# A hybrid decoder layer on one core: first expert index compared inside the sums, one-hot rows made by ACT, sample turns spread, first norm's gain on turned rows

## The chip, the cores and the metric

The kernel runs on one core of one Trainium2 chip. A core has a matrix engine (PE, with its weight loads shown as PEld), a vector engine (DVE), an activation engine (ACT), a general engine (POOL) that also issues the gathers, and SP, whose queue issues the plain DMAs. The metric is the device time of one execution in microseconds, the median of three: 2513.51 us before the change (2503.61 to 2522.33).

## The reference

One layer runs over 256 prompt tokens and over 8 x 4 sample tokens. The first half (projections, RWKV recurrence, sparse attention, output projection) isn't touched but for its end. What follows it:

```python
h = jnp.concatenate([y_r, y_n], axis=-1) @ p['w_out']
x = layer_norm(DEEPNORM_ALPHA * x + h, p['ln1_g'], p['ln1_b'])
f = peer_ffn(x, p['peer_wq'], p['peer_subkeys'], p['peer_u'], p['peer_v'])
x = layer_norm(DEEPNORM_ALPHA * x + f, p['ln2_g'], p['ln2_b'])
...
q = (xt @ wq).reshape(n, P_HEADS, 2, P_DKEY // 2)            # 8 heads, 2 halves of 128
s = jnp.einsum('nhcd,hckd->nhck', q, subkeys)                # 128 keys for each half
hv, hix = lax.top_k(s, P_TOPK)                               # 16 of 128
cand = (hv[:, :, 0, :, None] + hv[:, :, 1, None, :]).reshape(n, P_HEADS, 256)
cand_e = (hix[:, :, 0, :, None] * N_KEYS + hix[:, :, 1, None, :]).reshape(n, P_HEADS, 256)
tv, tpos = lax.top_k(cand, P_TOPK)
expert = jnp.take_along_axis(cand_e, tpos, axis=-1)          # 8 x 16 experts of 16384 a token
gate = jax.nn.softmax(tv, axis=-1)
h = jax.nn.gelu(jnp.einsum('cd,chkd->chk', xb, u_tab[eb]), approximate=False)
out = jnp.einsum('chk,chkd->cd', gb * h, v_tab[eb])
```

D is 2048, all in float32. An expert's number is 128 times a first index plus a second index, each 0 to 127.

## The kernel before

The program is written as stages; a scheduler sets the order of the instructions on each engine from its own estimate of times, held by priorities, by "issue after" marks and, in the weigh stage, by the order in which the source pins them. Tiles live in pools: a tile can be written when the tiles of its memory have been read for the last time, so the order in which pools open and close decides when a load may start. The stages that matter, with the times of the profiled execution:

- W4 (765 to 983 us): the prompt's attention, the first half of the output product (`out_first`, L1678), and the sample tokens' whole chain (`sample_chain`, L1465): their norm, queries, choice of experts, and their 64 gathered rows of `peer_u`, half a row of 1024 numbers each, in `cw` tiles, each multiplied and summed on DVE by one SCALAR_TENSOR_TENSOR with an accumulator (L1552, "sample dots").
- out (983 to 1062): the second half of the output product (`out_part(8, YN)`, L1647), with the sample dots woven into it (`weave((chain, 32), ...)`). DVE adds the product to x (L1676).
- ln1 (1062 to 1103): `layer_norm` (L1622) on 2 x 128 prompt tokens: bn_stats, a Newton rsqrt of small DVE steps for one block of tokens at a time, ACT's scaling of the rows (L1633), the gain on DVE (L1634), the bias half on POOL and half on DVE (L1635). PE turns the finished rows (L1727) and ACT copies them to `XT` (L1731). SP writes the rows to `X1D` in memory.
- wq (1103 to 1239): 16 column blocks of the query product (L1808, 32 matmuls each), ACT's copy to `QP` (L1809), scores (L1375) per head. `choose` (L1386) finds the best 16 of 54 candidate sums on DVE; POOL makes the candidates' numbers CE from HF and multiplies the hit mask by them (L1410); `settle` (L1413) adds the hits on DVE and writes the expert's number as an integer into GI, on DVE (L1417).
- peer/dense (1239 to 1713): for each first index i1, `dense` (L1837) multiplies 9 x 128 columns of x by the 128 experts' columns of u (AW holds all 16384 sums). The other 896 columns are gathered row by row for the chosen experts and summed on DVE (`dot`, L1771, one L1777 instruction a slot of 128 tokens, 256 slots in all). Gathered rows go through five tiles named `rows` (NRW = 5).
- weigh (1713 to 1982): 68 steps over 64 groups u of four tokens. `pick` (L1878): DVE compares an iota with both indices at once (`oo`, 128x1024), PE turns the second index's one-hot rows (tile pt) and ACT copies them (`oT`). `picked` (L1891): PE takes AW's rows (px). `product_of` (L1897): DVE multiplies px with the first index's one-hot rows and sums (four L1905 a step), ACT's Gelu every second step. `scaled` (L1915): ACT scales the first index's one-hot rows by the gate (four L1918). `put` (L1920): PE makes pa from the second index's rows and the scaled rows, ACT copies it into AW. In steps 0 to 27 the last 58 dots run. In steps 28 to 59 the sample's 64 gathers of `peer_v` go through the `rows` tiles, two a turn, and PE adds them into fs (L1942, eight matmuls a turn). After the steps the sample's second norm runs (its loads L1984 and L1986, L1987 on), and its 16 stores leave by SP (L1991).
- V (1982 to 2497): for 128 first indices k, `rows_load` (L1950) brings 1408 columns of v, ACT and DVE split them (L2034, L2035), PE multiplies by AW (L2042, 18 matmuls a k). The other 640 columns are gathered (`rq`) and added on DVE (L2015). From k = 66 on, every sixth k issues one load of the last norm's rows into AW's first half, which is read until then (L2056, L2060).

## Time and profile before

| stage | from, us | to, us | what bounds most of it |
|---|---|---|---|
| W4 | 765 | 983 | PE 202.82 of 218 busy |
| out | 983 | 1062 | DVE 70.96 and PE 59.73 of 79 |
| ln1 | 1062 | 1103 | DVE 37.00 of 41, PE 7.74 |
| wq | 1103 | 1239 | PE 123.42 and DVE 109.61 of 136 |
| dense | 1239 | 1713 | PE 462.09 of 474 |
| weigh, steps 0 to 27 | 1713 | 1840 | DVE 122.70 of 127 |
| weigh, the rest | 1840 | 1982 | PE 131.71 of 142 |
| V | 1982 | 2497 | PE 497.22 of 515 |

The profiled execution took 2521.09 us, its span 2518.9 us, and its mean granted clock of the matrix engine was 0.929. A stage's table says how long each engine was busy; whether an engine sets the stage's time is read from the waits and from the chain of work that ended last. An operation's mean time in a group holds its overlap with its neighbours, so for a row of many the busy time over the count is its pitch.

### The profile page before, as it was taken

The numbers are of one execution on the slowest core, as the hardware profiler recorded it, in microseconds if no ns is written. First come the engines' busy times: TensorE is split into PE (matmuls) and PEld (weight loads), VectorE is DVE, ScalarE is ACT, GpSimd is POOL, SyncE is SP. The second block draws the span as 40 slices with busy tenths as digits, with TensorE's granted clock in tenths as the row PEclk, the third lists the DMA queues.
The fourth block names the chain that finished last, engine by engine and source line by source line (L and its number), as shares of the span: only waits on it lengthen the run. The fifth ranks groups of instructions, "written<-read, shape, count | busy, mean of one in ns | idle before, by whom it ended". The sixth has DMA issues, their size and how long they took to land.

```text
span 2518.9 us, 44857 instructions
## 1 busy us (share of the span) xinstructions
...
## 2 busy tenths in 40 slices
...
GB/s 225 223 234 227 270 219 168 118 177 228 168 233 252 282 278 170 344 293 182 134 340 371 370 372 351 357 353 227 205 241 291 219 364 359 361 367 353 359 365 198
DMA packets 327420, 683.17 MB, mean 271 GB/s; under 512 B 82206, under 2 KB 200928, under 8 KB 326400
## 3 DMA queue, kind: packets, MB, share of 16 engines
...
q14 instruction: 91, 0.75, 0.1%
...
## 4 chain that ended last, share of the span: by engine, by line
PE 50%; DVE 17%; DMA 9%; POOL 9%; issue 8%; ACT 3%; SPq 1%; POOLq 0%; DVEq 0%; ACTq 0%
PE ph L1850 10%; PE pb L2042 10%; POOL rq L454 6%; PE pj L423 5%; PE ph L1843 3%; PE p L1080 2%; PE pa L1668 2%; DVE rows L1777 2%; PE pa L1924 2%; DVE ul L1640 2%; DMA co<-in_cache_cmp_kv,gidx 2%; PE pj L1808 1%; DVE cw L1552 1%; PE px L1894 1%; PE sa L921 1%
## 5 line engine op out<-in xcount | busy, mean ns | idle before, releaser
L454 POOL DMA_INDIRECT rq<-in_peer_v_g,gi x256 | 404.3, 1579 | 118.0 <-DVE fP L2015 67.8
L454 POOL DMA_INDIRECT rows<-in_peer_u_g,gi x256 | 327.0, 1277 | 249.5 <-DVE rows L1777 206.8
L1777 DVE SCALAR_TENSOR_TENSOR rows<-rows,x1a 128x896 f32<-128x896 f32 x256 | 274.3, 1100 | 2.0 <-DMA rows<-in_peer_u_g,gi 1.9
L423 PE MATMUL pj<-XH,wl 128*128 128x288 f32 (+1 forms) x752 | 231.8, 309 | 13.9 <-DVE wl L418 7.7
L423 PE MATMUL pj<-XH,wh 128*128 128x288 f32 (+1 forms) x752 | 229.7, 306 | 14.0 <-DVE ss L753 6.1
L1850 PE MATMUL ph<-XHd,uh 128*128 128x256 f32 x768 | 236.4, 308 | 0.0
L1850 PE MATMUL ph<-XHd,ul 128*128 128x256 f32 x768 | 224.6, 293 | 8.4 <-DVE ul L1640 3.6
L1640 DVE TENSOR_TENSOR ul<-ur,uh 128x384 fp32r<-128x384 f32 x256 | 133.6, 560 | 128.1 <-ACT uh L1639 88.1
L423 PE MATMUL pj<-XL,wh 128*128 128x288 f32 (+1 forms) x752 | 225.9, 301 | 0.0
L2015 DVE SCALAR_TENSOR_TENSOR fP<-rq,ge,fP 128x640 f32<-128x640 f32 x254 | 223.7, 881 | 2.4
L1850 PE MATMUL ph<-XLd,uh 128*128 128x256 f32 x768 | 217.0, 283 | 0.0
L2042 PE MATMUL pb<-vl,ah 128*128 128x512 f32 (+1 forms) x768 | 206.9, 378 | 0.0
L2042 PE MATMUL pb<-vh,ah 128*128 128x512 f32 (+1 forms) x768 | 187.7, 380 | 20.8 <-ACT vh L2034 20.8
L2042 PE MATMUL pb<-vh,al 128*128 128x512 f32 (+1 forms) x768 | 205.8, 376 | 0.0
L416 ACT CAST wh<-wraw 128x512 fp32r<-128x512 f32 (+1 forms) x188 | 115.0, 616 | 227.0 <-PE pj L423 188.3
L1843 PE MATMUL ph<-Xfd,ur 128*128 128x256 f32 x768 | 187.3, 379 | 2.4 <-DMA ur<-in_peer_u_t 2.4
L2042 PEld LDWEIGHTS pb<-vh,ah 128*128 128x128 f32 x768 | 142.9, 191 | 44.5 <-ACT vh L2034 21.9
L477 DVE SCALAR_TENSOR_TENSOR CA<-co,wbc,CA 128x256 f32<-128x256 f32 x248 | 135.6, 585 | 48.5 <-DMA co<-in_cache_cmp_kv,gidx 48.5
L1850 PEld LDWEIGHTS ph<-XHd,ul 128*128 128x128 f32 x768 | 146.5, 191 | 22.7 <-DVE ul L1640 22.0
L423 PEld LDWEIGHTS pj<-XH,wl 128*128 128x128 f32 (+1 forms) x752 | 143.9, 191 | 25.7 <-DVE wl L418 11.6
L1852 ACT COPY AW<-ph 128x256 f32<-128x256 f32 x128 | 77.8, 608 | 217.4 <-PE ph L1850 204.8
L423 PEld LDWEIGHTS pj<-XH,wh 128*128 128x128 f32 (+1 forms) x752 | 144.2, 192 | 20.7 <-ACT wh L416 6.7
...
## 6 DMA issues: line engine op xcount, KB each, us to landing
ur<-in_peer_u_t SPq DMA_DIRECT2D x128, 576.0 KB
...
wraw<-in_w_in SPq DMA_DIRECT2D x64, 128.0 KB
...
```

The costliest lines, as they stand in the source:

```text
L416: sc.copy(wh[:, :, :n], w[:, :, :n])
L423: last[2] = pe.matmul(pb[:n, :nt], wi[:, k, :n], xi[(o + k) // 8][:, (o + k) % 8, :nt], start=(o + k == 0 and wi is wh and xi is xh), stop ...
L454: gp.indirect_dma_start(out=dst, out_offset=None, in_=rows_, in_offset=bass.IndirectOffsetOnAxis(ap=ix, axis=0))
L477: ve.scalar_tensor_tensor(d_, x_, w_, d_, op0=OP.mult, op1=OP.add)
L1080: pe.matmul(pb[hs[c], 64 * m:64 * m + 64], lhs(hs[c], m), rhs(hs[c], m), start=True, stop=True)
L1640: return ve.tensor_tensor(xl, pb, xh.bitcast(F32), OP.subtract)
L1777: i_ = ve.scalar_tensor_tensor(r_, r_, 1.0, X1a[t][:, :UG], op0=OP.mult, op1=OP.mult, accum_out=h_)
L1843: pe.matmul(ph[:, :NPR], w[:, e, :], Xfd[:, e - NSP, :], start=(e == NSP), stop=False)
L1850: mm = pe.matmul(ph[:, :NPR], wi[:, e - e0, :], xi[:, e, :], start=False, stop=(e == NSP - 1 and wi is wl))
L1852: return lo_, mm, sc.copy(AW[:, i1 // 64, :, i1 % 64], ph[:, :NPR])
L2015: ve.scalar_tensor_tensor(fP[t], r_, w_, fP[t], op0=OP.mult, op1=OP.add)
L2042: pe.matmul(acc[3 * t + q][:, :n_], wi[:, P * t:P * t + P], xi[:, 512 * q:512 * q + n_], start=(k == 0 and wi is ah and xi is vh), stop=(k ...
```

## The change

1. Weigh: the one-hot rows of the second index alone are made (`onehot`, two steps ahead): for u under 32 by ACT, four Square of (index - iota) and one Relu of (1 - 2 x square); for later u by DVE, one compare of 128x512. `product_of` compares the iota with the first index inside the SCALAR_TENSOR_TENSOR. `scaled` moves from ACT to DVE: a TENSOR_SCALAR compares and multiplies by the gate, into tiles `rs`.
2. Weigh: the sample's 32 turns go to steps 5 to 59, seven steps to four turns, their gathers two steps ahead; dots fetch two ahead rather than five. The sample's norm loads start at step 44 into the tile of `X1a`, the norm stands at step 61.
3. The first norm: bn_stats move into `out_part`, the rsqrt runs once for both token blocks, DVE scales and shifts the rows (eight TENSOR_SCALAR of 128x512), PE turns them, and ACT applies gain and bias on the turned rows as per-partition operands (32 activations of 128x128). The rows written to `X1D` get gain (DVE) and bias (POOL) afterwards, and POOL's queue stores them. The split `XH`, `XL` is made later from `XT`.
4. The sample's dots: 14 of 32 turns stay in the out stage, whose product gets priority 400; 36 dots go behind the normed rows, through five own tiles `sr`, 4 behind each `choose` of the first six heads.
5. wq: the first query loads are issued ahead, X1a is loaded at h = 2; HF comes straight from HI; `settle` writes the integer by POOL.
6. Pools: order of opening in W4 (on SP, peer_wq's first loads move behind x_prompt's), in weigh and in V; in V each late load stands behind that k's `rows_load`.

```diff
@@ -33,6 +33,8 @@
 NSO = 4
+NSD = 14
+NLD = 6
@@ -51,6 +53,7 @@
 NRW = 5
+UA = 32
...
@@ -1389,8 +1393,9 @@
             top16(S[:, c, :], HV[:, c, :], HI[:, c, :])
-        gp.tensor_copy(HF, HI)
-        gp.tensor_scalar(HF[:, 0], HF[:, 0], 128.0, None, op0=OP.mult)
+        k_ = 2.0 if t == 2 else 1.0
+        for c in range(2):
+            gp.tensor_scalar(HF[:, c], HI[:, c], k_ if c else k_ * P, 0.0, op0=OP.mult, op1=OP.add)
@@ -1412,9 +1417,9 @@
         ve.tensor_reduce(EF, hit, AX.X, OP.add)
-        ve.tensor_scalar(GI[t][:, 16 * h:16 * h + 16], EF, 2.0 if t == 2 else 1.0, None, op0=OP.mult)
+        gp.tensor_copy(GI[t][:, 16 * h:16 * h + 16], EF)
@@ -1539,18 +1544,24 @@
             ve.tensor_scalar(IG, GI[2], 1.0, None, op0=OP.add)
-        for s_ in range(32):
+        yield from sample_dots(ring, x4, 0, NSD)
+    def sample_dots(ring, x4, n0, n1):
+        for s_ in range(n0, n1):
             yield 1
+    def sample_formed():
...
@@ -1674,6 +1675,7 @@
                     ve.tensor_tensor(x_, x_, acc[t], OP.add)
+                    ve.bn_stats(out=lst[:, t, cq, :], in_=x_)
@@ -1700,15 +1702,25 @@
     weave((take(chain, 38), 38), (prompt_attention(), 19), (out_first(), 19))
-    weave((chain, 32), (out_part(8, YN), 16))
+    weave((chain, NSD), (out_part(8, YN), 16, 400))
-    XH, XL = (xq([P, NSP, NPR], nm, F32R) for nm in ("XHq", "XLq"))
+    kw_ = Pool("kw", "right")
+    wring = lambda: kw_([P, 8, P], "wraw", bufs=WB)
+    def query_load(c, o):
...
+    wq_ = {(0, o): query_load(0, o) for o in (0, 8)}
@@ -1717,25 +1729,39 @@
     for t in range(2):
-        layer_norm(lp, lambda c0, n: x1c(t, c0, n),
...
-            sy.dma_start(X1D[P * t:P * t + P, 1024 * hf:1024 * hf + 1024], X1[t][hf])
+        ve.bn_aggr(out=lmv[:, t, :], in_=lst[:, t].rearrange("p a b -> p (a b)"))
+    ve.tensor_scalar(lv, lmv[:, :, 1], 1e-5, None, op0=OP.add)
+    rsqrt(lp, lrr, lv, "ln")
+    ve.scalar_tensor_tensor(lv, lmv[:, :, 0], -1.0, lrr, op0=OP.mult, op1=OP.mult)
+    for t in range(2):
         for q in range(4):
+            x_ = x1c(t, 512 * q, 512)
+            normed = ve.tensor_scalar(x_, x_, lrr[:, t:t + 1], lv[:, t:t + 1], op0=OP.mult, op1=OP.add)
                 pe.transpose(pb[:, 128 * e:128 * e + 128], x1c(t, 512 * q + 128 * e, 128), ident)
...
+            for e in range(4):
...
+                sc.activation(XT[:, k, P * t:P * t + P], pb[:, 128 * e:128 * e + 128], AF.Identity,
+                              bias=prm("ln1_b", 16, k), scale=prm("ln1_g", 16, k))
+    sq_ = Pool("sq", "right")
...
+    late = sample_dots(lambda: sq_([P, 1024], "sr", bufs=5), sx4, NSD, 32)
+    with tc.issue_after(normed.ins):
+        for _ in take(late, NLD):
+            pass
+        for hf in range(2):
+            for t in range(2):
+                for nm, op_ in (("ln1_g", OP.mult), ("ln1_b", OP.add)):
+                    for q in range(2):
+                        x_, y_ = (t_[:, 512 * q:512 * q + 512] for t_ in (X1[t][hf], gb1[nm, hf]))
+                        (ve if op_ is OP.mult else gp).tensor_tensor(x_, x_, y_, op_)
+                gp.dma_start(X1D[P * t:P * t + P, 1024 * hf:1024 * hf + 1024], X1[t][hf])
@@ -1745,13 +1771,14 @@
-    X1a = [up([P, UG], f"x1a{t}") for t in range(2)]
...
+    xa_ = up([P, 2 * UG], "x1a")
+    X1a = [xa_[:, UG * t:UG * t + UG] for t in range(2)]
...
@@ -1802,13 +1828,15 @@
                 for o in range(0, 16, 8):
...
+                    w = wq_.pop((c, o), None) or query_load(c, o)
                         pe.matmul(pb[:, :NPR], w[:, k, :], XT[:, o + k, :], start=(o + k == 0), stop=(o + k == 15))
-                sc.copy(QP[:, c, :], pb[:, :NPR])
+                last_ = sc.copy(QP[:, c, :], pb[:, :NPR])
                 S = [scores(t, h - 1, kc, QP, SKT, "pb") for t in range(2)]
+        if h == 2:
+            for t in range(2):
+                sy.dma_start(X1a[t], X1D[P * t:P * t + P, :UG])
@@ -1817,13 +1845,22 @@
                     settle(t, h - 2, kc, hit)
-                if h > 2:
+                for _ in take(late, 2):
+                    pass
+                if h > 6:
         settle(t, 7, kc, hit)
+    with tc.issue_after(chosen.ins), tc.issue_after(last_.ins):
+        for _ in late:
+            pass
+        sample_formed()
+    sq_.close()
     kw_.close()
-    sc.copy(XHd, XH)
-    sc.copy(XLd, XL)
+    for q in range(NSP // 2):
+        k2, x_ = slice(2 * q, 2 * q + 2), XT[:, 16 - NDB + 2 * q:18 - NDB + 2 * q, :]
+        sc.copy(XHd[:, k2, :], x_)
+        gp.tensor_tensor(XLd[:, k2, :], x_, XHd[:, k2, :].bitcast(F32), OP.subtract)
...
@@ -1872,18 +1909,26 @@
-    hot, prod, act = {}, {}, {}
+    hot, prod, act, rate = {}, {}, {}, {}
+    def onehot(u):
+        oo = hot[u] = x4p([P, 4, P], "oo", bufs=7)
+        if u < UA:
+            sq = x4p([P, 4, P], "sq", bufs=2)
+            for e in range(4):
+                pin(sc.activation(sq[:, e, :], iota, AF.Square, bias=TB[:, 1, 4 * u + e:4 * u + e + 1], scale=-1.0))
+            pin(sc.activation(oo, sq, AF.Relu, bias=one, scale=-2.0))
+        else:
+            pin(ve.tensor_tensor(oo, iota[:, None, :].to_broadcast([P, 4, P]),
+                                 TB[:, 1, 4 * u:4 * u + 4, None].to_broadcast([P, 4, P]), OP.is_equal))
-        tk = slice(4 * u, 4 * u + 4)
-        oo = hot[u] = x4p([P, 2, 4, P], "oo", bufs=6)
-        pin(ve.tensor_tensor(oo, iota[:, None, None, :].to_broadcast([P, 2, 4, P]),
-                             TB[:, 0:2, tk, None].to_broadcast([P, 2, 4, P]), OP.is_equal))
         for e in range(4):
-            pin(pe.transpose(pb[:, 128 * e:128 * e + 128], oo[:, 1, e, :], ident))
+            pin(pe.transpose(pb[:, 128 * e:128 * e + 128], hot[u][:, e, :], ident))
@@ -1896,14 +1941,14 @@
-        px, o1 = prod.pop(u), hot[u][:, 0]
+        px = prod.pop(u)
             xj, n_ = x4p([P, P], "xj"), 4 * (u % 2) + e
-            pin(ve.scalar_tensor_tensor(xj, px[:, 128 * e:128 * e + 128], 1.0, o1[:, e, :], op0=OP.mult, op1=OP.mult,
-                                        accum_out=E[:, n_:n_ + 1]))
+            pin(ve.scalar_tensor_tensor(xj, iota, TB[:, 0, 4 * u + e:4 * u + e + 1], px[:, 128 * e:128 * e + 128],
+                                        op0=OP.is_equal, op1=OP.mult, accum_out=E[:, n_:n_ + 1]))
@@ -1913,22 +1958,28 @@
     def scaled(u):
+        rs = rate[u] = x4p([P, 4, P], "rs", bufs=3)
         for e in range(4):
-            o_ = hot[u][:, 0, e, :]
-            pin(sc.activation(o_, o_, AF.Copy, scale=TB[:, 2, 4 * u + e:4 * u + e + 1]))
+            n_ = 4 * u + e
+            pin(ve.tensor_scalar(rs[:, e, :], iota, TB[:, 0, n_:n_ + 1], TB[:, 2, n_:n_ + 1], op0=OP.is_equal, op1=OP.mult))
     def put(u):
-        oo = hot.pop(u)
+        oo, rs = hot.pop(u), rate.pop(u)
         for e in range(4):
-            pin(pe.matmul(pa[:, 128 * e:128 * e + 128], oo[:, 1, e, :], oo[:, 0, e, :], start=True, stop=True))
+            pin(pe.matmul(pa[:, 128 * e:128 * e + 128], oo[:, e, :], rs[:, e, :], start=True, stop=True))
     ve.tensor_tensor(ws, C0("sum4")[:, None, :32].to_broadcast([P, 32, 32]), GE[2][:, :, None].to_broadcast([P, 32, 32]), OP.mult)
@@ -1947,9 +1998,12 @@
     left = 2 * P - got[1]
+    turns = {5 + j * 7 // 4: j for j in range(32)}
+    for u in range(2):
+        onehot(u)
@@ -1964,37 +2018,43 @@
             product_of(s_ - 1)
+        if s_ + 2 < 64:
+            onehot(s_ + 2)
         if s_ < 28:
-            dot(-(-left * (s_ + 1) // 28) + 2 * P - left - got[1], keep=True)
-        elif s_ < 60:
-            smp_fetch(s_ - 28)
-        if 30 <= s_ < 62:
-            smp_add(s_ - 30)
+            dot(-(-left * (s_ + 1) // 28) + 2 * P - left - got[1], keep=True, ahead=2)
+        if s_ + 2 in turns:
+            smp_fetch(turns[s_ + 2])
+        if s_ in turns:
+            smp_add(turns[s_])
+        if s_ == 44:
+            bs_, gs_, x_ = (xa_[:, 512 * n:512 * n + 512] for n in range(3))
...
             rows_load(0)
+        if s_ == 61:
+            ve.scalar_tensor_tensor(x_, x_, ALPHA, fs, op0=OP.mult, op1=OP.add)
+            norm_quarters(x4p, x_, gs_, bs_, "pb")
...
...
     vp = Pool("vp", "left")
+    vp([P, FD], "v_", bufs=2)
+    vp([P, FD], "vh", F32R, bufs=2)
     fP = [vp([P, VG], f"fP{t}") for t in range(2)]
+    vp([P, VG], "rq", bufs=NRQ)
@@ -2034,7 +2094,7 @@
         if k + 3 < P:
-            rows_load(k + 3)
+            ld_ = rows_load(k + 3)
@@ -2049,15 +2109,16 @@
         if 66 <= k < 114 and k % 6 == 0:
...
+            with tc.issue_after(ld_.ins):
...
```

Three places where instructions move, as the program orders them. First, DVE from the first norm's Newton steps on, before (x_00 to x_11 are the rows of x, token block and half; cw the sample's gathered rows, XLq the split of the turned rows):

```order
L1552 SCALAR_TENSOR_TENSOR cw,hd<-cw,x_10488 128x1024
L245 TENSOR_TENSOR ln_t<-lnrr 128x1
L1634 TENSOR_TENSOR x_00_9703<-x_00_9703,wraw 128x512
L246 SCALAR_TENSOR_TENSOR ln_t<-ln_t,lnmv 128x1
L1552 SCALAR_TENSOR_TENSOR cw,hd<-cw,x_10488 128x1024
L1634 TENSOR_TENSOR x_00_9703<-x_00_9703,wraw 128x512
L1635 TENSOR_TENSOR x_00_9703<-x_00_9703,wraw 128x512
L247 SCALAR_TENSOR_TENSOR lnrr<-ln_t,lnrr 128x1
```

and with the change (sr are the sample's gathered rows, shT the tile their sums lie in):

```order
L1735 SCALAR_TENSOR_TENSOR lnv<-lnmv,lnrr 128x2
L1739 TENSOR_SCALAR x_00_9713<-x_00_9713,lnrr,lnv 128x512 x2
L1739 TENSOR_SCALAR x_01_9714<-x_01_9714,lnrr,lnv 128x512 x2
L1739 TENSOR_SCALAR x_10_9715<-x_10_9715,lnrr,lnv 128x512 x2
L1739 TENSOR_SCALAR x_11_9716<-x_11_9716,lnrr,lnv 128x512 x2
L1560 SCALAR_TENSOR_TENSOR sr,shT<-sr,sx_12077 128x1024 x5
L1760 TENSOR_TENSOR x_00_9713<-x_00_9713,wraw 128x512 x2
```

The sample's dots no longer stand between the norm's steps; the gain on the rows stands behind the rows that PE turns.

Second, DVE in a step of weigh while dots run, before and then with the change (xj is a scratch tile, E the sums, TB the table of indices and gates turned to tokens):

```order
L1882 TENSOR_TENSOR oo<-CT_61,TB 128x1024
L1905 SCALAR_TENSOR_TENSOR xj,E<-px,oo 128x128 x4
L1908 TENSOR_TENSOR E<-E,TB 128x8
L1777 SCALAR_TENSOR_TENSOR rows,hd_12213<-rows,x1a_12209 128x896 x2
L1882 TENSOR_TENSOR oo<-CT_61,TB 128x1024
```

```order
L1953 TENSOR_TENSOR E<-E,TB 128x8
L1804 SCALAR_TENSOR_TENSOR rows,hd_12151<-rows,x1a 128x896 x2
L1958 TENSOR_TENSOR TB<-E,TB 128x8
L1964 TENSOR_SCALAR rs<-CT_61,TB 128x128 x4
L1950 SCALAR_TENSOR_TENSOR xj,E<-CT_61,TB,px 128x128 x4
```

The compare of 1024 columns is gone from DVE here, and four scalings stand in its place. POOL's gathers in the same steps, which before were 250 of `peer_u_g` in a row with all of `peer_v` behind them, now read:

```order
L458 DMA rows<-in_peer_u_g,gi_71 128x896 x4
L458 DMA rows<-in_peer_v,gi_72 128x1024
L458 DMA rows<-in_peer_v,ig 128x1024
L458 DMA rows<-in_peer_u_g,gi_71 128x896 x5
L458 DMA rows<-in_peer_v,gi_72 128x1024
```

Two gathers of a sample turn stand between four or five of the dots', in the same five tiles.

Third, SP's queue in V, before and then with the change (v_ is a load of v's rows, AW the tile that the last norm's rows go into):

```order
L1950 DMA v__22831<-in_peer_v 128x1408
L2056 DMA AW<-x1d 128x1024 x4
L2060 DMA AW<-in_ln_g 128x1024 x2
L1950 DMA v__22861<-in_peer_v 128x1408
L2060 DMA AW<-in_ln_b 128x1024 x2
L1950 DMA v__22895<-in_peer_v 128x1408
```

```order
L2001 DMA v__23273<-in_peer_v 128x1408
L2117 DMA AW<-x1d 128x1024
L2001 DMA v__23304<-in_peer_v 128x1408
L2001 DMA v__23338<-in_peer_v 128x1408
L2001 DMA v__23368<-in_peer_v 128x1408
```

Eight loads that stood between three loads of v now stand one by one, six loads of v apart.

More of the change, by code (lines that the diff above doesn't have):

```diff
@@ L1604, in hybrid_decode_step @@
     more_banks(sa=2, pb=1, sao=1, pa=2)
+    lp = Pool("lp", "left")
+    cx = [Pool("cx", "left")]
+    oe = Pool("oe", "left")
+    for nm, n_ in [(f"Y{c_}{q}", 1) for q in range(0, 8, 2) for c_ in "HL"] + [("wh", 2), ("wl", 2)]:
+        oe([P, 2, 512] if n_ > 1 else [P, 2, NPR], nm, F32R, bufs=n_)
     np_ = Pool("np", "left")
```

100 lines of the change are left out of this document (41 added, 59 removed).

## The prediction

> **What bounds the kernel now.** I read the stretches of the program first, each engine's busy time in each, because one mean over the span mixes stages with different limits.
>
> ```profile
> core 0: us, PE busy (x) PEld busy (x) DVE busy (x) ACT busy (x) POOL busy (x), PEclk, DMA share, GB/s
> 765.00:983.00 218.00, 202.82 (x1284) 133.09 (x1285) 97.13 (x364) 67.94 (x193) 40.88 (x67) 0.81 0.74 251
> 983.00:1062.00 79.00, 59.73 (x236) 44.94 (x234) 70.96 (x104) 21.93 (x31) 58.73 (x41) 0.84 0.89 320
> 1062.00:1103.00 41.00, 7.74 (x31) 5.77 (x31) 37.00 (x79) 10.45 (x19) 27.05 (x22) 0.55 0.79 274
> 1103.00:1239.00 136.00, 123.42 (x581) 108.35 (x581) 109.61 (x481) 19.37 (x44) 68.70 (x116) 0.94 0.64 198
> 1239.00:1713.00 474.00, 462.09 (x3077) 422.65 (x3075) 349.15 (x752) 184.85 (x387) 270.19 (x228) 1.00 0.93 347
> 1713.00:1840.00 127.00, 85.92 (x523) 78.45 (x524) 122.70 (x386) 60.73 (x162) 71.26 (x56) 0.78 0.70 211
> 1840.00:1955.00 115.00, 112.37 (x890) 80.87 (x889) 82.19 (x332) 78.77 (x215) 68.54 (x60) 1.00 0.81 275
> 1955.00:1982.00 27.00, 19.34 (x133) 15.14 (x131) 15.20 (x67) 18.65 (x48) 3.34 (x4) 0.91 0.35 101
> 1982.00:2497.00 515.00, 497.22 (x2304) 426.39 (x2304) 482.40 (x460) 240.84 (x190) 401.91 (x254) 0.97 0.95 349
> ```
>
> PE is the bound in five of them. It is nearly idle in the first norm (7.74 of 41 us), waits for DVE in the first 28 steps of weigh (85.92 of 127) and stands for 7.66 us in 1955 to 1982. Dense (PE 462 of 474) keeps its matmuls, so the change can only pay in the others.
>
> **W4 and out.** On SP four loads of peer_wq now stand behind x_prompt. Before, they held the queue:
>
> ```profile
> 770.77 11.47 SPq L1806 DMA_DIRECT2D wraw<-in_peer_wq  x4
> 796.10 2.07 PE L1695 MATMUL pa<-sg,wraw 128*128 128x256 f32 x4 [0.87 <-DMA wraw<-in_rwkv_g]
> ```
>
> PE saw only 0.87 us of that. I take -2, between 0 and -8 (PE's clock in the stage is 0.81, so an earlier start could shift more). In out, DVE is the fuller engine, by the sample's dots:
>
> ```profile
> L1552 DVE SCALAR_TENSOR_TENSOR cw<-cw,x 128x1024 f32<-128x1024 f32 x33 | 47.3, 1451 | 8.0 <-DMA cw<-in_peer_u,ig 5.2 <-DMA cw<-in_peer_u,gi 2.7
> PE pa L1668 <- DVE wl L1663: 6.9, 8, 2.8
> ```
>
> With 28 dots at most and the product at a higher priority, PE's 6.9 us of waiting for wl is what can go: -6, between 0 and -12.
>
> **First norm.** The stage is a chain on DVE, in which single Newton steps of 0.17 us stand in line with sample dots, and the dots wait for gathers:
>
> ```profile
> 1066.30 0.19 DVE lnmv L1436 x2
> ...
> 1068.32 0.16 DVE lnrr L247
> ...
> 1081.33 7.96 DMA cw<-in_peer_u,gi
> L1634 DVE TENSOR_TENSOR x<-x,wraw 128x512 f32<-128x512 f32 x8 | 8.2, 1041 | 0.9 <-ACT x L1633 0.9
> L1727 PE MATMUL pa<-CT,x 128*128 128x128 f32 x31 | 8.2, 431 | 34.0 <-DVE x L1635 32.6 <-POOL x L1635 1.4
> ```
>
> The second block's Newton steps are cut in two by the 7.96 us that a gathered row took to arrive, and PE's transposes wait 32.6 us for the last add of the rows. With the change no dot stands ahead of the rows that PE turns, and gain and bias leave the chain. What is left from the last add of x (1062.5): statistics 0.9, Newton 2.2 (1066.30 to 1068.48), the first TENSOR_SCALAR of 512 some 0.6 (0.4 to 1.0, the row of L1634 above), four transposes about 1, then ACT's 32 activations of 128 columns. The nearest row is weigh's scaling of the same shape (L1918, quoted below): 30.7 us for 96, a pitch of 0.32, so 10.2; with a second operand up to its whole 0.39, 12.5. In all 15 to 17.5, so the query product begins near 1078 where it began at 1103.2: -25, between -18 and -28. The gain's eight TENSOR_TENSORs (8.2) and POOL's adds follow beside the query product; nobody waits for X1D before h = 2.
>
> **Query stage.** PE stood here, for one reason:
>
> ```profile
> ACT QP L1809: 25.5, 2
> 1122.02 6.95 DMA cw<-in_peer_u,ig
> 1103.00:1131.00 28.00, 16.03 (x67) 13.57 (x66) 19.30 (x35) 3.06 (x6) 12.80 (x11) 0.80 0.96 326
> L1363 DVE MAX8 HV<-TB 128x8 f32<-128x128 f32 x24 | 5.7, 280 | 9.2 <-ACT TB L1383 9.2
> L1417 DVE TENSOR_SCALAR gi<-EF 128x16 int32<-128x16 f32 x8 | 9.2, 1154 | 0.2
> ```
>
> The 25.5 us count the weight load and the matmul, so PE lost 12.7 (the window shows 12.0 idle). ACT's copies of QP stood behind the sample's Gelu, which waited for the last dots, and these for their gathers (6.95). The Gelu now stands behind all copies: -12.7. Against it, DVE gets four sample dots in each of six heads. From 1130 to 1230 it passed six heads; without its idle time, its dots and the 9.2 us of L1417 (which goes to POOL) about 11 us a head remain; with four dots of 1.24 it is 16, and PE's head is 15.3 (135 us less 12.7, over eight). So DVE becomes the bound by 0.7 us a head. Twelve dots (15 us) and the gains (8) stand ahead of the first choice, which then begins about 1095, and the eighth about 1095 + 6 x 16 + 12 = 1203. PE ends the query product near 1078 + 121 = 1199 and has three halves of ul for dense, 5.5 us; the fourth comes within the eighth choice. A stall of 3 to 8 is in store. -8 for the stage, between -13 and +10 (POOL, with the hits, four gathers and the integer write, late too).
>
> **Weigh.** The rows of both phases:
>
> ```profile
> L454 POOL DMA_INDIRECT rows<-in_peer_u_g,gi x51 | 64.3, 1261 | 49.8 <-DVE rows L1777 42.1 <-issue 7.0 <-DVE xj L1905 0.6
> L1777 DVE SCALAR_TENSOR_TENSOR rows<-rows,x1a 128x896 f32<-128x896 f32 x54 | 56.6, 1086 | 0.0
> L1882 DVE TENSOR_TENSOR oo<-CT,TB 128x1024 f32<-128x1024 f32 x26 | 31.7, 1221 | 0.0
> L1918 ACT ACTIVATE oo<-oo,TB 128x128 f32<-128x128 f32 x96 | 30.7, 393 | 0.0
> L1905 DVE SCALAR_TENSOR_TENSOR xj<-px,oo 128x128 f32<-128x128 f32 x104 | 30.1, 289 | 2.9 <-PE px L1894 0.2
> L1942 PE MATMUL fs<-rows,ws 128*32 128x512 f32 x240 | 33.8, 605 | 0.0
> 1951.31 0.59 PE pt L1886 x4
> 1951.90 0.89 PE pa L1924 x8
> 1952.79 1.00 PE px L1894 x8
> ...
> 1955.16 4.01 DMA rows<-x1d
> 1959.18 4.70 DMA rows<-in_ln_b
> ```
>
> Steps 0 to 27 took 127 us, 4.5 a step, all DVE's. From a step go 1.22 of oo (L1882); four scalings of 128 columns come. No row shows them: below, a share of L1905's 0.29 without its accumulator, 0.12, above 0.29 each; I take 0.19, 0.75 a step. With 62 dots for 58, DVE's step is about 4.2. ACT's step is then four Squares (1.3), a Relu of 512 (0.6, as the copies of that size), two copies (1.2): 3.1, still under it. POOL gets 0.57 turns of two gathers beside 2.2 dots, 2.8 gathers of 1.26 and 0.3 between them: 4.4 a step. Its 42.1 us of waiting for DVE say that there is room, so 28 x 4.4 = 123. But five tiles now hold dots and sample rows together, a sample row for two steps, and a tile's turn waits for the fifth before it. A gather took 7 to 8 us to arrive above; here DVE waited 0.0 for its rows with five tiles to itself. I add 15: 138, +11; bounds -4 and +35.
>
> From step 28 on, PE's step is 0.59 + 0.89 + 1.00 + 0.99 for fs = 3.47. Fourteen of the 32 turns have gone, so a mean step is 2.48 + 0.5 x 1.0 = 3.0, DVE near 2.8 (1.2 of sums, 0.75, half of oo 0.61, the rest small). Over 36 steps 0.45 each: -16, and the 8.7 us in which the matmuls stood for the norm's loads (4.01 and 4.70) go as well, since these start at step 44. Against it the sample's norm now stands among DVE's last steps: +4. Together -21, between -32 and -10. Weigh: -10.
>
> The Trainium skill ("ScalarE: Activation LUTs", Rules for kernel authors) speaks against this part: relu and other cheap element work belongs on VectorE, which is faster. Kept there, half of oo would cost DVE 0.61 a step in the stretch where the rows show DVE full and ACT busy for 60.73 of 127, so by that rule the first phase would be 17 us longer on DVE; the trace's engine load decides, and I go by it.
>
> **V.** One stall stands out:
>
> ```profile
> PE pb L2042 <- ACT vh L2034: 17.1, 2, 11.7
> 2224.23 2.64 SPq L2056 DMA_DIRECT2D AW<-x1d  x4
> ...
> 2228.13 0.40 SPq L1950 DMA_DIRECT2D v__22861<-in_peer_v  x1
> 2230.28 3.17 SPq L2060 DMA_DIRECT2D AW<-in_ln_b  x2
> 2249.35 2.72 PE L2042 MATMUL pb<-vh,ah 128*128 128x512 f32 x6 [11.69 <-ACT vh L2034]
> ```
>
> Eight late loads issue at once ahead of two of v, PE waits 11.69 and restarts at a clock of half. They are now spread. The other 5.4 us of waits at the start (v behind the 16 stores of the sample's norm, whose tiles it reused) go in part. PE is busy for 497 of 515 and DMA for 0.95, so no more than -18 is there; the transfers that ran in the stall must run elsewhere. -14, between -5 and -18.
>
> **Sum.** -2 - 6 - 25 - 8 - 10 - 14 = -65, from the profiled 2521.09 to 2456. That execution was 7.6 above the median of the runs, so the forecast is 2448.5.
>
> **Rivals.** (a) Weigh's first phase hangs on the five tiles: a tile freed by a sample turn is issued 1.5 us later and arrives 7.5 us after, for a dot 1.5 steps on, so a step takes 9 / 1.5 = 6.0 and the 28 make 168: weigh +20 instead of -10, 2478.5. For it speaks the landing of 7 to 8 us, against it POOL's 42.1 us of waiting. (b) DVE late in the query stage: dense waits for ul through the eighth choice, +10 instead of -8: 2466.5. (c) All hidden: weigh -36 (first phase -4, second -32), out -12, V -18: 2412.5. Phase one's DVE sum speaks for it. (d) Slower: POOL works in order, so a gather that waits for a sample row's tile holds all dots behind it; if each step then pays one issue and one landing in full, 1.5 + 8 (1081.33 and what its issue took), the 28 steps cost 266, 139 more than before, in place of my +11: 2576.5. It decides from 7.25 us a step on, where the 28 steps cost 203 and the other gains of 76 are gone. (e) The moves come to nothing, for example by new waits in ln1 for XT: 2505.
>
> **How the numbers follow.** Forecast 0.45, (a) 0.16, (b) 0.12, (c) 0.15, (d) 0.07, (e) 0.05. One per cent, 25 us, is about what a measurement tells from no change. Faster by more than that are all but (d) and (e): 0.88. Within it lie (e) and, at 6.4 to 8.1 us a step, a share of (d) of 0.02: 0.07; slower the rest of (d): 0.05. The range holds the forecast, (a), (b) and (c) with their terms' bounds: 2406 to 2492.
>
> **What would show it.** First query matmul 25 us earlier than the last x add now allows, PE's transposes behind TENSOR_SCALAR and not behind adds; no wait of the matmuls for QP; in weigh's first 28 steps, DVE at 4.2 to 5 us a step with waits for gathers of rows, PE at 3.0 after them; no 11.7 us stall in V. Wrong would make it: steps over 6 us in weigh, or a wait of dense for ul over 15 us.

## The result and the profile after

The changed kernel took 2540.32 us (median of six runs, 2534.49 to 2549.7), the kernel before 2510.38 beside it: a ratio of 1.0107 (95% interval 1.0077 to 1.0136). It is slower by 1.1 per cent. That is 92 us above the forecast of 2448.5 and outside its range of 2406 to 2492. The profiled execution of the changed kernel has a span of 2541.1 us, 22.2 more than the one before.

The changed kernel's busy times by stretch, in the columns of the table in the prediction (first norm 1062 to 1072, query product to 1199, dense to 1693, steps 0 to 27 of weigh to 1859, the rest to 1998, V to 2521):

```profile
core 0: us, PE busy (x) PEld busy (x) DVE busy (x) ACT busy (x) POOL busy (x), PEclk, DMA share, GB/s
...
1062.00:1072.00 10.00, 6.03 (x32) 5.79 (x32) 9.58 (x27) 5.94 (x18) 2.23 (x2) 0.66 0.03 4
1072.00:1199.00 127.00, 120.56 (x577) 106.19 (x578) 116.94 (x400) 19.53 (x53) 97.41 (x133) 0.97 0.89 280
1199.00:1693.00 494.00, 462.37 (x3078) 422.76 (x3076) 370.34 (x850) 184.48 (x390) 281.86 (x256) 0.98 0.90 337
1693.00:1859.00 166.00, 111.94 (x646) 85.48 (x646) 125.68 (x450) 86.92 (x216) 94.30 (x86) 0.78 0.77 256
1859.00:1998.00 139.00, 117.29 (x897) 94.47 (x897) 125.77 (x565) 52.82 (x112) 38.37 (x39) 0.96 0.48 156
1998.00:2521.00 523.00, 505.35 (x2304) 429.34 (x2304) 484.90 (x463) 239.61 (x191) 386.78 (x254) 0.98 0.93 341
```

PE's busy time in dense is the 462 us of before, in a stretch 20 us longer; DVE's in steps 0 to 27 is 125.68 for 122.70 before, in a stretch of 166 for 127. DVE's work hardly grew there; its waiting did. PE's 26 us and POOL's 23 us more in that stretch are the sample's turns, which came into it. By the first and last instruction of each stage:

| stage | before, us | changed, us | forecast | came |
|---|---|---|---|---|
| up to the last add of x | 1061.9 | 1060.0 | -8 | -1.9 |
| first norm, to the first query matmul | 41.3 | 12.2 | -25 | -29.1 |
| query product and dense | 608.3 | 619.8 | -8 | +11.5 |
| weigh, to V's first matmul | 270.6 | 306.1 | -10 | +35.5 |
| V's matmuls | 514.0 | 520.3 | -14 | +6.3 |
| end | 22.8 | 22.7 | 0 | -0.1 |

The first row can't be told from chance: in kernels with the same code up to there the last add of x began between 1037.9 and 1064.7. All that follows is read by stage. Of the 87 us between the forecast of -65 and the +22.2 of the two profiled executions, weigh has 45.5, V 20.3, the query stage and dense 19.5 and the first row 6.1; the first norm gave 4.1 more than forecast.

The first norm went as forecast. Its groups of instructions in the changed kernel (1060 to 1080):

```profile
L1745 ACT ACTIVATE XT<-pa,PT 128x128 f32<-128x128 f32 x32 | 11.3, 552 | 12.8 <-PE pa L1742 12.8
...
L1742 PE MATMUL pa<-CT,x 128*128 128x128 f32 x32 | 6.0, 377 | 5.8 <-DVE x L1739 5.8
...
L1739 DVE TENSOR_SCALAR x<-x,lnrr,lnv 128x512 f32<-128x512 f32 x8 | 3.7, 542 | 0.0
```

PE's transposes wait 5.8 us for the first scaled rows, where they waited 32.6 for an add, and ACT's 32 activations take 0.35 apiece. They run from 1066.1 to 1077.4, and the first query matmul starts at 1072.2, beside them.

**Dense begins late.** For dense, each block of u is split into a high part `uh`, made by ACT, and a low part `ul`, made by DVE. PE's waits from 1199 to 1240 in the changed kernel, then lines of its DVE timeline and one of ACT's:

```profile
PE ph L1887 <- DVE ul L1641: 22.7, 1, 22.7
```

```profile
1073.69 13.21 DVE L1760 TENSOR_TENSOR x<-x,wraw 128x512 f32<-128x512 f32 x8
...
1106.90 0.65 ACT L1387 COPY TB<-pb 128x256 f32<-128x256 f32 x2 [13.35 <-DMA x1d<-x]
1107.30 0.87 DVE L1367 MAX8 HV<-TB 128x8 f32<-128x128 f32 x4 [4.09 <-ACT TB L1387]
...
1134.95 2.02 DVE L1413 TENSOR_TENSOR rows<-CT,TF 128x864 f32<-128x864 f32 x2
...
1138.81 2.78 DVE L1560 SCALAR_TENSOR_TENSOR sr<-sr,sx 128x1024 f32<-128x1024 f32 x1
...
1152.39 2.02 DVE L1413 TENSOR_TENSOR rows<-CT,TF 128x864 f32<-128x864 f32 x2
```

The first choice begins at 1107.3, not 1095. The gains took 13.2 us and not 8.2; two of the dots behind them took 2.3 us rather than 1.2, and two more waited 3.3 and 2.7 us for their gathers; then DVE waited 4.1 us for the score table TB from ACT, which waited for the store of x whose memory it takes. A head takes 17.4 us (1134.95 to 1152.39) and not 16, as the first dot of each four takes 2.8 us beside POOL's product of the hits. So dense, with three ul in hand, stands 22.7 us for the fourth.

Of the gains, one alone makes the difference. The shortest, median and longest of the eight in ns, and POOL's timeline:

```profile
L1760 DVE TENSOR_TENSOR x<-x,wraw x8: 680/684/8911, 1073.7 to 1086.2; 128x512 f32<-128x512 f32 x8
```

```profile
1077.71 6.15 POOL L1760 TENSOR_TENSOR x<-x,wraw 128x512 f32<-128x512 f32 x5
1083.82 0.62 POOL L1761 DMA_DIRECT2D x1d<-x  x1
1084.46 1.28 POOL L1760 TENSOR_TENSOR x<-x,wraw 128x512 f32<-128x512 f32 x1
```

The seventh gain, begun at 1077.4, stood through POOL's first six adds of the bias and ended at 1086.3, 0.6 us after the sixth.

**Weigh's first 28 steps.** DVE's groups in the changed kernel, 1697 to 1859:

```profile
L1804 DVE SCALAR_TENSOR_TENSOR rows<-rows,x1a 128x896 f32<-128x896 f32 x57 | 61.4, 1089 | 32.8 <-DMA rows<-in_peer_u_g,gi 25.9 <-PE pt L1931 3.7 <-PE fs L1993 3.2
L1950 DVE SCALAR_TENSOR_TENSOR xj<-CT,TB,px 128x128 f32<-128x128 f32 x104 | 36.0, 346 | 6.6 <-PE px L1939 3.8
L1964 DVE TENSOR_SCALAR rs<-CT,TB 128x128 f32<-128x128 f32 x96 | 27.6, 369 | 0.4
```

The dots wait 32.8 us, most of it for their gathered rows, where the row of before had 0.0. And rs costs 0.29 apiece (27.6 over 96), the upper bound of the estimate, not 0.19. The sums (xj) with the compare inside take 36.0 us for 104, where they took 30.1 before.

**V.** Here vh and vl are the high and low part of a row block of v, ah and al those of AW for a pair of k; ACT casts vh and ah, DVE makes vl and al. The heap of late loads is gone, but ACT's and PE's timelines show a new pattern at each of the eight spread loads:

```profile
2260.13 1.16 ACT L2091 CAST ah<-AW 128x512 fp32r<-128x512 f32 x1 [1.73 <-PE pb L2102]
2261.18 1.38 ACT L2094 CAST vh<-v__23273 128x1408 fp32r<-128x1408 f32 x1
2267.78 1.08 ACT L2091 CAST ah<-AW 128x512 fp32r<-128x512 f32 x1 [5.22 <-issue]
2268.76 1.36 ACT L2094 CAST vh<-v__23304 128x1408 fp32r<-128x1408 f32 x1
```

```profile
2260.57 1.44 PE L2102 MATMUL pb<-vh,ah 128*128 128x512 f32 x6
...
2266.95 0.80 PE L2102 MATMUL pb<-vl,ah 128*128 128x512 f32 x3
2267.58 0.80 PE L2102 MATMUL pb<-vh,al 128*128 128x512 f32 x3
2270.18 1.89 PE L2102 MATMUL pb<-vh,ah 128*128 128x512 f32 x6 [1.80 <-ACT vh L2094]
```

PE starts a pair at 2260.57, before the ah of 2260.13 is done, so that ah is for the next pair and the one of 2267.78 for the pair after it. This last one needs the buffer of the ah in use, which PE reads for the last time in the products with vl that end at 2267.75 (2266.95 and 0.80; the view puts the wait down to "issue"); behind it, in ACT's order, stands the vh that PE needs at once. Before a spread load the program's order on ACT is vh, vh, ah. At it, an ah has moved ahead of a vh:

```
L2094 CAST vh<-v__23209 128x1408
L2094 CAST vh<-v__23239 128x1408
L2091 CAST ah<-AW 128x512
L2094 CAST vh<-v__23273 128x1408
L2091 CAST ah<-AW 128x512
L2094 CAST vh<-v__23304 128x1408
L2094 CAST vh<-v__23338 128x1408
```

### The profile page after: what moved, and what is told of

Read it like the earlier page. It is cut to its first block, busy times and chain, and to the rows that moved or that the text cites. A ratio compares the mean times of both kernels' runs of the same rounds, so it can differ in the third digit from the quotient of the medians.

```text
span 2541.1 us, 44943 instructions
## 1 busy us (share of the span) xinstructions
PE 2260.4 (89%) x16396; PEld 1891.4 (74%) x16396; DVE 1899.8 (75%) x4458; ACT 937.8 (37%) x1760; POOL 1365.2 (54%) x1422
## 4 chain that ended last, share of the span: by engine, by line
PE 29%; DVE 15%; DMA 6%; issue 5%; ACT 3%; POOL 1%; DVEq 0%; SPq 0%; ACTq 0%; POOLq 0%
PE pb L2102 16%; PE ph L1887 9%; PE ph L1880 3%; DVE xj L1950 3%; DMA ur<-in_peer_u_t 2%; DVE rs L1964 2%; DMA rows<-in_peer_u_g,gi 2%; DVE sr L1560 2%; DVE ul L1641 1%; DVE rows L1804 1%; ACT uh L1640 1%; DVE vl L2095 1%; ACT vh L2094 1%; PE px L1939 1%; DVE rows L1413 1%
## 5 line engine op out<-in xcount | busy, mean ns | idle before, releaser
L458 POOL DMA_INDIRECT rq<-in_peer_v_g,gi x256 | 389.1, 1520 | 151.7 <-DVE fP L2075 88.2
L458 POOL DMA_INDIRECT rows<-in_peer_u_g,gi x256 | 317.9, 1242 | 240.7 <-DVE rows L1804 184.4
L2102 PE MATMUL pb<-vh,ah 128*128 128x512 f32 (+1 forms) x768 | 187.2, 379 | 17.3 <-ACT vh L2094 14.4
L2102 PEld LDWEIGHTS pb<-vh,ah 128*128 128x128 f32 x768 | 141.6, 189 | 43.1 <-ACT vh L2094 17.4
L2102 PEld LDWEIGHTS pb<-vl,ah 128*128 128x128 f32 x768 | 144.2, 194 | 27.2 <-DVE vl L2095 4.4
L427 PEld LDWEIGHTS pj<-XH,wl 128*128 128x128 f32 (+1 forms) x752 | 146.2, 194 | 22.3 <-DVE wl L422 8.5
```

The costliest lines, as they stand in the source:

```text
L427: last[2] = pe.matmul(pb[:n, :nt], wi[:, k, :n], xi[(o + k) // 8][:, (o + k) % 8, :nt], start=(o + k == 0 and wi is wh and xi is xh), stop ...
L458: gp.indirect_dma_start(out=dst, out_offset=None, in_=rows_, in_offset=bass.IndirectOffsetOnAxis(ap=ix, axis=0))
L2102: pe.matmul(acc[3 * t + q][:, :n_], wi[:, P * t:P * t + P], xi[:, 512 * q:512 * q + n_], start=(k == 0 and wi is ah and xi is vh), stop=(k ...
```

## Experiments

All kernels below are the changed kernel with the edits shown, but for one of the kernel before. Times of stages run from first to last instruction. "Steps 0 to 27" and "28 to 63" are taken from ACT's copies of oT.

**What slows weigh: ACT's queue or the shared tiles.** In the changed kernel the Gelu also waits long for DVE, with ACT's Squares behind it, so there were two theories.

```diff
-        if 0 <= s_ - 1 < 64:
-            product_of(s_ - 1)
         if s_ + 2 < 64:
             onehot(s_ + 2)
+        if 0 <= s_ - 1 < 64:
+            product_of(s_ - 1)
```

> Edit: in each weigh step the one-hot rows of the group two ahead are made before the products, so that on ACT the four Squares and the Relu stand ahead of the Gelu that waits for DVE's sums, not behind it. The changed kernel took 162.5 us from the first to the twenty-ninth copy of oT (steps 0 to 27) and 126.3 us for steps 28 to 63. Theory A (ACT's queue: the Gelu holds Squares, Relu and the next oT copy, so each pair of steps is one closed loop of DVE, ACT and PE): steps 0 to 27 fall to 130 to 140. Theory B (the five row tiles shared by dots and sample rows make DVE wait for gathers): 155 to 165, no change. V and the query stage as in the changed kernel under both.

Measured: 162.4 us for steps 0 to 27, no change, and 130.5 for the rest, 4.2 longer.

```diff
-UA = 32
+UA = 0
```

> Edit: DVE makes the second index's one-hot rows in all 64 groups (UA = 0), ACT none. Theory A (ACT's queue): steps 0 to 27 fall from 162.5 to 135 to 145, although DVE gets 0.6 us more a step. Theory B (row tiles): 160 to 175, since DVE has more to do and still waits for gathers.

Measured: 166.2. Theory A falls: without any Square on ACT the steps are as slow.

```diff
-    turns = {5 + j * 7 // 4: j for j in range(32)}
+    turns = {30 + j: j for j in range(32)}
...
-        if s_ == 61:
+        if s_ == 62:
```

> Edit: the sample's 32 turns go back to one a step, steps 30 to 61, with the sample's norm at step 62; the dots have the five row tiles to themselves in steps 0 to 27, ACT still makes the one-hot rows. Theory B (row tiles): steps 0 to 27 fall from 162.5 to 125 to 135, and DVE's wait for gathers there goes. Theory A (ACT's queue): 155 to 162. Under both steps 28 to 63 rise by some 5 to 10 us, because PE gets a turn in every step.

Measured: 130.7 and 129.7; 2506.6 us in all in its one run, the kernel before 2498.4 beside it. DVE's dots in this kernel, 1690 to 1815, wait for nothing:

```profile
L1804 DVE SCALAR_TENSOR_TENSOR rows<-rows,x1a 128x896 f32<-128x896 f32 x57 | 59.6, 1086 | 0.0
```

So the spread is the cause. Whether through the time that a sample row holds one of the five tiles, or through the work of 30 more gathers there, two more kernels tell (both with the edit of V's casts that follows, too):

```diff
-        if s_ + 2 in turns:
-            smp_fetch(turns[s_ + 2])
+        if s_ + 1 in turns:
+            smp_fetch(turns[s_ + 1])
```

> The changed kernel with V's casts held in order and the sample's turns spread over steps 5 to 59 as in the change, but each turn's two gathers fetched one step ahead rather than two: a sample row holds its tile about half as long, while POOL and the DMAs have the same work. If the hold of the shared tiles is what slows steps 0 to 27 (164 us with two steps ahead, 130.5 with no turns there): 140 to 152. If the work of POOL's gathers or of the DMAs is: 160 to 166.

Measured: 158.3.

```diff
-        if s_ + 2 in turns:
-            smp_fetch(turns[s_ + 2])
+        if s_ + 3 in turns:
+            smp_fetch(turns[s_ + 3])
```

> The same kernel with the gathers of a turn fetched three steps ahead: a sample row holds its tile half as long again. If the hold of the tiles is the cause: steps 0 to 27 rise from 164 to 175 to 200. If the work of POOL or of the DMAs is: 160 to 166, as the work is the same.

Measured: 205.9. With the same work, a step more of holding cost 42 us, and a step less saved 5.5, under the 12 to 24 expected (against 163.8 us in the kernel with the edit of V's casts alone). DVE's busy time in these stretches is nearly the same in all (124.56 of 129 before, 123.22 of 162 changed, 124.31 of 131 late, 126.88 of 158 one step ahead, 127.18 of 205 three ahead), and so is POOL's in the three spread ones (90.91, 95.28, 89.54). So it isn't the amount of work, but how far ahead a sample row takes its tile. A gather issued earlier also stands earlier in POOL's queue; these two weren't separated.

With one step ahead the kernel is still 28 us above the one without turns there. PE's waits in its steps 0 to 27 show a new one, for the sample's rows to land before PE adds them into fs:

```profile
PE fs L1993 <- DMA rows<-in_peer_v,gi: 15.5, 8, 3.4
PE fs L1993 <- DMA rows<-in_peer_v,ig: 5.6, 9, 1.2
```

In the changed kernel such waits came to 0.8 us. How much of the 28 they make isn't separated. Fewer or more shared tiles, or tiles of the sample's own, were not tried, so that this part stays open.

**V: the casts' order or the loads.**

```diff
+        pin(sc.copy(vh, v_))
         if k % 2 == 0:
...
-            sc.copy(a2[0], aw_)
+            pin(sc.copy(a2[0], aw_))
...
-        sc.copy(vh, v_)
```

> Edit: ACT's casts in V are held in one order, vh of the even k, then ah, then vh of the odd k. In the changed kernel this order is broken at each of the eight late loads: ah stands ahead of a vh there, waits 5.2 us for PE, and PE then waits 1.8 us for that vh and runs at a lower clock. V's matmuls took 520 us from first to last, against 511.5 before. Theory C (the order on ACT): 498 to 503, no wait of over 1 us in the middle of V. Theory D (the DMAs are full, and 4 MB of late loads cost their 11.7 us wherever they stand): 510 to 520, and the waits remain, at a transfer of v.

Measured: 497.5 us, 22.8 less than in the changed kernel, with the loads at their places. PE's waits in V then and in the changed kernel:

```profile
PE pb L2102 <- ACT ah L2092: 5.2, 4, 2.9
PE pb L2102 <- DVE vl L2095: 0.7, 1, 0.7
```

```profile
PE pb L2102 <- ACT vh L2094: 14.4, 8, 1.8
```

PE's gaps in V come to 15.3 us in the changed kernel, 14.4 of them these eight waits, and to 3.2 in this one (the 2.9 above stands ahead of V's first matmul): 12 of the 22.8. The rest is slower work, as the same 2304 matmuls kept PE busy for 505.3 us and for 494.6. From the first wait on, in the changed kernel:

```profile
core 0: us, PE busy (x) PEld busy (x) DVE busy (x) ACT busy (x) POOL busy (x), PEclk, DMA share, GB/s
...
2271.20:2274.60 3.40, 3.40 (x10) 2.65 (x9) 3.37 (x4) 0.19 (x1) 1.48 (x1) 0.50 0.97 363
2274.61:2298.40 23.79, 22.00 (x102) 18.33 (x101) 21.18 (x22) 11.20 (x9) 16.39 (x11) 1.00 0.96 355
```

After six of the eight waits the granted clock is 0.50 for 3.4 us, and the 24 matmuls behind the wait take 6.8 to 7.3 us, where 24 without a wait ahead take 5.1. After the other two (at 2351.0 and 2456.8) it stays at 1.00, and they take 5.6. Why these two were spared isn't shown.

```diff
-            sc.copy(a2[0], aw_)
+            pin(sc.copy(a2[0], aw_))
...
-        sc.copy(vh, v_)
+        pin(sc.copy(vh, v_))
```

> The changed kernel with ACT's casts in V held in the order of the source, ah before both vh of its pair, in all 64 pairs (the sample's turns as in the changed kernel). Theory C (the order on ACT makes the stall): every pair then pays what the eight broken places pay, some 3 us (1.8 of waiting and a lower clock), so V takes 497 + 56 to 64 x 2 to 3 = 620 to 690. If the stalls came from the late loads themselves (theory D), V stays at 515 to 525.

Measured: 499.5. I had read the ah at the broken place as that of the same pair, and expected ah ahead of vh to cost in every pair. It costs nothing there; what costs is the ah of the pair after next ahead of a vh, and any fixed order by k excludes that. Theory D falls with it. In all 13 kernels of the changed form with these casts held, V takes 496 to 503 us; in the four without, 520 to 521.

The pin of vh ahead of ah in the kernel before:

```diff
+        pin(sc.copy(vh, v_))
         if k % 2 == 0:
...
-            sc.copy(a2[0], aw_)
+            pin(sc.copy(a2[0], aw_))
...
-        sc.copy(vh, v_)
```

> The kernel before, with nothing but V's casts on ACT held as vh, ah, vh. SP still issues the eight late loads in three heaps between three loads of v. If the order on ACT alone made its stall of 11.7 us: V takes 498 to 503 us rather than 514. If the heap of loads made it, by the late loads of v: 508 to 514, with one wait of 8 us or more for a load of v.

Measured: 514.4, as without it (514.0). PE's waits in V in that kernel:

```profile
PE pb L2042 <- ACT ah L2032: 10.3, 1, 10.3
PE pb L2042 <- ACT vh L2028: 6.5, 1, 6.5
```

ACT waits 14.1 us there for one load of v. Before the change the heap of loads was the cause; spread and with the casts in order, V takes 16.5 us less.

**Both together, and the query stage.** First the late turns (30 + j, and 62) with vh pinned ahead of ah:

> Two edits together, each seen alone: the sample's turns in steps 30 to 61 and ACT's casts in V held as vh, ah, vh. If the two causes are separate, steps 0 to 27 take 130 to 132 us and V 497 to 500, and the time is 50 to 58 us below the changed kernel and 20 to 35 below the kernel before. If one gain was only time moved from one stage to the other, less than 45 below the changed kernel.

Measured: 130.4 us for steps 0 to 27, V 498.9, 2488.96 us in all (ratio to the kernel before 0.9892, 0.9829 to 0.9956). The two gains add. The next kernels have both edits.

```diff
-NSD = 14
+NSD = 32
```

> As the kernel with both edits, and all 32 sample turns of dots run from the chain that belongs to the out stage (NSD = 32), so that none stands behind the choices of the first six heads. Theory E (the 24 dots between the choices make DVE's head 17.4 us, the eighth choice late and dense stand 23 us for ul): the wait for ul falls under 8 us and dense from first to last matmul goes from 492 to 474 to 480; ln1 or the first choice may become 5 to 15 us longer. Theory F (dense stands because the first choice begins late, at 35 us after the first query matmul, for the stores of x and the gains): the wait for ul stays above 15 us.

```diff
-NSD = 14
+NSD = 22
```

> As the kernel with both edits, with 22 of 32 turns of the sample's dots in the out stage: 8 dots rather than 24 stand between the choices, behind the first two heads alone. Theory E: the wait for ul falls by 16 x 1.6 = 25 us at most, to under 8 us. Theory F: it stays above 15.

Measured: waits for ul of 2.5 and 2.8 us and dense at 472.2 and 470.6, but the query stage at 168.9 and 152.2 for 126.0: PE waited 49.1 and 33.2 us for the load of SKT, the subkeys of the scores, whose memory the dots' rows still held. 2513.97 (0.9974, 0.9938 to 1.001) and 2503.7. That stall gives DVE the time it lacked, so neither kernel tells E from F.

```diff
-                for _ in take(late, 2):
-                    pass
...
-        for _ in late:
-            pass
```

> As the kernel with the sample's turns late and V's casts held in order, with the 24 of the sample's 64 dots that stand between the choices, and their gathers, left out (the sample tokens' output lacks them). Theory E (these dots make DVE's head 17.4 us and dense late): the head falls to 11 to 13 us of DVE, PE's wait for ul from 22 to under 5, and the query stage and dense together from 617.6 us to 595 to 600. Theory F (the late first choice is enough to do it): PE still waits over 10 us for ul. No store, gain or table is moved.

Measured: dense 471.2, PE's wait for ul 2.9 us, query stage and dense 598.5 for 617.6, though the first choice still waits for its gains and tables. So the 24 dots with their gathers cost 19 us of query stage and dense (the lengths of the two added), as theory E has it. Not all of it is the head: that fell from 17.4 to 14.7 us and not to 11 to 13, and the first choice came 29.8 us behind the first query matmul, for 34.4 with the dots.

```diff
-NSD = 14
+NSD = 16
```

> The same kernel with 16 rather than 14 of the sample's 32 turns of dots in the out stage (4 dots fewer between the choices; nothing spills behind the norm in the program's order). Theory E: the wait for ul falls by 4 x 1.6 = 6 us, and out stays within 2 us, as DVE had 18 us of room there. Otherwise: no change of the wait.

Measured: wait for ul 19.1 for 22.3, dense 488.6 for 491.6: -3, half of what was expected; 2473.3 us in its one run.

Then weigh's arithmetic as before the change, with the late turns, the pinned casts and NSD = 16:

```diff
-    def onehot(u):
...
+        oo = hot[u] = x4p([P, 2, 4, P], "oo", bufs=6)
...
-            pin(ve.scalar_tensor_tensor(xj, iota, TB[:, 0, 4 * u + e:4 * u + e + 1], px[:, 128 * e:128 * e + 128],
-                                        op0=OP.is_equal, op1=OP.mult, accum_out=E[:, n_:n_ + 1]))
+            pin(ve.scalar_tensor_tensor(xj, px[:, 128 * e:128 * e + 128], 1.0, o1[:, e, :], op0=OP.mult, op1=OP.mult,
+                                        accum_out=E[:, n_:n_ + 1]))
...
-            pin(ve.tensor_scalar(rs[:, e, :], iota, TB[:, 0, n_:n_ + 1], TB[:, 2, n_:n_ + 1], op0=OP.is_equal, op1=OP.mult))
+            pin(sc.activation(o_, o_, AF.Copy, scale=TB[:, 2, 4 * u + e:4 * u + e + 1]))
```

> The same kernel with 16 turns in out and with weigh's arithmetic as before the change (DVE compares both indices in one 128x1024 instruction, ACT scales), the sample's norm and its loads as in the change. If moving compares and scaling between DVE and ACT brought nothing, as DVE's rows say (TENSOR_SCALAR 0.28 a piece, not 0.19): steps 0 to 27 at 126 to 131 us and steps 28 to 63 at 118 to 126, against 130.4 and 130.2, and the time 5 to 20 us under the 2489 of the kernel with both edits. If the new form was worth something: longer by 3 us or more in either phase.

Measured: 133.6 and 129.3, and 2473.57 (0.988, 0.9846 to 0.9915) in nine runs. The old form is 2.9 us longer in the first phase and 0.8 shorter in the second; from dense's end to V it is 280.8 us for 279.7, one trace each. The new form is worth some 1 to 3 us, then, and not 10; the times as a whole (2473.57 and 2473.3) don't tell the two apart.

Two more edits on top of NSD = 16, first both, then UA alone:

```diff
-UA = 32
+UA = 27
...
-                        (ve if op_ is OP.mult else gp).tensor_tensor(x_, x_, y_, op_)
+                        ve.tensor_tensor(x_, x_, y_, op_)
```

> The kernel with late turns, casts in order and 16 turns of dots in out, with two small edits in two stages. First, the bias on the rows for memory is added by DVE rather than POOL (the eight gains took 13.2 us on DVE beside POOL's adds, 8.2 before): if the two engines slow each other there, the first choice begins earlier and the wait for ul falls by 3 to 6 us from 19.1; if not, DVE's eight extra adds make it longer by 5. Second, ACT makes one-hot rows only for groups under 27 (UA = 27): steps 28 to 31, 15.5 us, become 12 to 13.

> The same without the bias on DVE: late turns, casts in order, 16 turns of dots in out, UA = 27. Steps 28 to 31 at 12 to 13 us as above; as a whole 3 us under the kernel without the last edit, 1.3 to 2.2 per cent under the kernel before.

Measured: with both, the wait for ul is 11.4 and dense 479.9; with UA = 27 alone 18.2 and 487.8. The 16 TENSOR_TENSORs on DVE took 10.1 us, where eight beside POOL's adds took 13.2. The first choice came 27.4 us behind the first query matmul for 34.0 with UA = 27 alone, and the wait for ul fell by as much. So theory F has a part too: while the dots stand between the choices, what delays the first choice delays dense. Steps 28 to 31 became longer, not shorter (18.7 in both, for 15.5), so UA = 27 isn't kept; why is open. With UA = 27 alone 2492.65 (0.989, 0.9851 to 0.9928), 1.1 per cent under the kernel before and not 1.3 to 2.2.

Last, late turns, pinned casts, NSD = 16 and the adds on DVE:

```diff
-NSD = 14
+NSD = 16
...
-    turns = {5 + j * 7 // 4: j for j in range(32)}
+    turns = {30 + j: j for j in range(32)}
...
-                        (ve if op_ is OP.mult else gp).tensor_tensor(x_, x_, y_, op_)
+                        ve.tensor_tensor(x_, x_, y_, op_)
...
+        pin(sc.copy(vh, v_))
```

> Four edits of the changed kernel: turns in steps 30 to 61, casts of V in order, 16 turns of dots in out, the bias for memory on DVE (UA back to 32). From the stages of the kernels that had them alone: 2489 for the two first, less 3 to 5 for the dots, less 8 for the bias, so 2474 to 2480 where the kernel before takes 2504 to 2520: 1.3 to 2.0 per cent under it.

Measured: 2482.52 us in six runs (2472.83 to 2489.55), the kernel before 2513.17: 0.9882 (0.9847 to 0.9918). Steps 0 to 27 take 130.7 us in it, V 499.6, and the wait for ul is 7.3. It beats the kernel before by 1.2 per cent, for 1.3 to 2.0 expected, and lies far below the changed kernel's runs, the shortest of which took 2534.49; the 2 to 8 us over the expected time lie within what the runs of one kernel differ by. Nor is it told apart from the kernel with weigh's old arithmetic, whose ratio was 0.988.

## Why the prediction was wrong, step by step

- **First norm, -25: right in mechanism, in part by luck in size.** -29.1, just past the bound of -28. The chain was read rightly: the adds and the Newton steps between dots, and what is left of it. But the sum put all of ACT's activations (10.2 us) ahead of the first query matmul, which came 6.1 us behind the first of them. The way from the last add's end to that first one took 5.4 us, where 4.7 were summed.
- **Query stage, -8 with bounds to +10: wrong in size,** +11.5, and this is rival (b), +10: dense stood for ul through the eighth choice. The step "with four dots of 1.24 it is 16" took each dot at its price alone, and the gains at the 8.2 us of a row in which only two of eight had stood beside a POOL add (2.07 and 2.15 us for 0.68). Beside POOL's two-input work the first dot took 2.8, and one gain 8.91. That DVE becomes the bound and the eighth choice is late was said; the stall of 3 to 8 was 22.7. Leaving out the dots removes it.
- **Weigh's first phase, +11: wrong in size,** +34, at the place that rival (a) named, the five tiles. The step "I add 15" had no row behind it. POOL's 42 us of waiting for DVE, taken there as room, was time in which all five tiles were full: with no turns POOL waits 48.6 us there and the steps take 130.7. That rival (a)'s 6.0 us a step came near the 5.8 measured is in part luck: its 1.5 + 7.5 us over 1.5 steps doesn't contain how far ahead a sample row takes its tile, and this alone moved the step from 5.65 to 7.35. Rival (d) was to decide from 7.25 us a step on, which only three steps ahead reached; its own 9.5 came nowhere.
- **DVE's step of 4.2: wrong.** The late kernel shows what weigh's arithmetic is worth without waits: 130.7 for 128.5. The sums were left at their old price without a reason and grew by 5.9 us (36.0 for 30.1); with the 27.6 of rs and three to four more dots they took back the 31.7 that oo gave.
- **Weigh's second phase, -21: wrong.** +2.4 from step 28 to 63, and +1.0 from step 28 to V. The steps fell from 3.58 to 3.26 us between 32 and 60. PE's 3.0 came as 3.07, but DVE's 2.8 as 3.1 (1.4 of sums, 1.1 of rs, 0.7 of oo), and DVE was busy for 87.2 of these 91.3 us, PE for 85.9. The first four steps still waited for tiles (19.7 us for 11.8); and the sample's norm in the last steps cost what its load wait had cost (28.1 us from step 60 to V for 26.3).
- **V, -14: the loads were read rightly, the result was not.** Spreading them is worth 16.5 us, as the pinned kernel and the unpinned one before show. The step failed at "They are now spread": with the loads' places ACT's casts moved too, in the program's order that was there to be read, and V came out at +6.3. No rival held it.
- The rule of the Trainium skill ("ScalarE: Activation LUTs", Rules for kernel authors) that cheap element work belongs on VectorE was set aside by the row of engine load. The kernel with all compares on DVE took 166.2 us in the first phase, four kernels with ACT's compares and the same turns 162.4 to 164.9. As the tiles set the time in all five, this doesn't test the rule; the 17 us stay an estimate.
